# A decoder layer on one core: seven edits at the places where the matmul engine stops

## The chip, the cores and the metric

The kernel runs on one core of a Trainium2 chip. Its engines are named as in the profile: PE multiplies matrices, PEld loads its weights, DVE, ACT and POOL are the vector, scalar and general engines, SP issues transfers. The metric is the device time in microseconds (µs), the median of several executions. Times inside the program are counted from the start of the profiled span.

## The reference

One step of a hybrid decoder layer for 512 prompt tokens and 64 sample tokens (8 sequences of 8), all in float32, width 1024:

```python
u = _rms(x) * g_pre_mix
z, xbc, dt_raw, q, k, v, ig, fg, og = split(u @ w_in)
y_ssd = ssd_scan(silu(causal_conv(xbc)), softplus(dt_raw), ...)    # Mamba-2
h_ml = mlstm_scan(q, k, v, ig, log_sigmoid(fg), ...)               # gates per token
x = x + _rms(concat(y_ssd, h_ml) @ w_out) * g_post_mix
u = _rms(x) * g_pre_x
pr = softmax(einsum(u @ w_xq, mem_k))
x = x + _rms(einsum(pr, mem_v) @ w_xo) * g_post_x
u = _rms(x) * g_pre_ffn
x = x + _rms((silu(u @ w_gate) * (u @ w_up)) @ w_down) * g_post_ffn
```

`_rms(x)` divides each token's row by the root of its mean square. The outputs are x of both groups, the memory's keys and values, and the new states.

## The kernel before, in words

**Layout.** Activations lie with features on the 128 partitions and the 576 tokens (512 and 64) along the rows, eight blocks of 128 features. Tokens are taken in two halves, 256 and 320 (in the later stages 288 and 288), one bank of accumulators each.

**Products.** A float32 product is three matmuls of a reduced 32-bit format: high part by high part, high by low, low by high. A weight arrives by DMA in `raw` or `rawx`; ACT copies it to `whi` (the rounding copy is the high part), and DVE or POOL subtracts to get `wlo`; in other places ACT writes the negated high part and a DMA of POOL adds the weight to it (`wacc`, `wlo`). `split` (L196 on) is a cast on ACT and a subtraction on DVE, `split_w` (L178 on) does it for a weight with its load.

**Start.** 19 matmuls of zeros (`NWARM`, L309) run while the first loads are under way. Then, for each of eight blocks k, ACT makes `uh` and DVE `ul` from x (`xraw`), and two weight units `wi[0]`, `wi[1]` are split. For k = 0 x comes in two halves, and the weights are split behind both.

**Mixer.** The gates of the mLSTM are rows of 4 partitions that DVE and ACT work on beside the projection's matmuls; they are copied into one tile `r` (L545 to L567), which PE turns into columns (`ps_ct`, L589). In the state-space part, DVE makes `lm` from `ps_l`, ACT takes exponentials (L674), DVE multiplies (L675) and PE takes the product (`ps_yi`, L682). The mLSTM's values of the samples, `vts`, are taken out of their bank by a copy on ACT and an addition on DVE (L877, L878).

**Cross attention's output.** `xo` multiplies one block of features; `out` takes the squares for the norm and the scaled copy out of the bank, both on ACT (L270, L1560). PE writes the block three further on into the bank that is freed last.

**Feed-forward.** Products of two by two blocks take seven instead of eight part products (classes `Seven`, `Pair` for gate and up, `Down`), with sums of weights in `sw`: `parts2` casts a sum to `whi<-sw` on ACT and subtracts on DVE. The last 768 columns of the down projection are kept per block j in `wdh` and `wdl` (`w_of`).

**Tail.** The last stage is a list of steps with a place each (`at_`, then `plan.sort()`), issued in that order. `evac0(j)` adds a bank to `f_ffn`, squares it on ACT and scales it; `root` sums the squares over the partitions by matmuls with ones (`ps_ss`, one column per block of 128 tokens) and takes the square root on ACT, `root_end` refines it on DVE; `last` adds the scaled, transposed block to x and stores it; the last block is scaled on ACT and added on DVE (`scaled`, `scaled_add`).

**What sets the order.** Up to the tail, a scheduler orders each engine's instructions by its own simulated timeline, within what `issue_after` and priorities force. A small edit can so move instructions far from it. Each engine executes its own list in order.

Of the kernel before, what the change touches and what calls it, by code (L numbers as in the profile page):

```python
# [19 lines left out]
P = 128  # L20
T = 576
# [87 lines left out]
CCUT = 128  # L109
NWARM = 19  # L110
NSS = 7
# [4 lines left out]
def build(nc, tc, ctx, I, O):  # L116
# [52 lines left out]

    loads, casts, accs = [], [], []  # L170

# [5 lines left out]

    def split_w(src, n=1024, cut=CUT, acc=False, pool=None, to=None, raw=None):  # L178
# [89 lines left out]
    def add_sq(pool, ssq, src, j, w=T, eng=None, t0=0, q=None):  # L268
        if j == 0:
            A.activation(ssq[:, t0:t0 + w], src, AF.Square)  # L270
# [45 lines left out]
    for k in range(KT):  # L316
# [7 lines left out]
        if k == 0:  # L324
            with tc.issue_after(xd.ins), tc.high_priority(offset=300):

                A.activation(sp.tile([P, 1], F32, name="one"), wz[:, 0:1], AF.Exp)

        if k == 0:
            V.tensor_copy(wi[0][0][:, c], raws[0][:, c])  # L330
        for t0, n in ([(0, T)] if k else HALVES):
            ts_ = slice(t0, t0 + n)
            uhk = A.activation(uh[:, k, ts_], xraw[:, k, ts_], AF.Copy, scale=PAR("g_pre", k))
            ulk = V.scalar_tensor_tensor(ul[:, k, ts_], xraw[:, k, ts_], PAR("g_pre", k), uh[:, k, ts_].bitcast(F32),
                                         op0=ALU.mult, op1=ALU.subtract)
        if k % 2 == 0:
            for i in range(2):
                with tc.issue_after(uhk.ins), tc.issue_after(ulk.ins):
                    split(wi[i][0][:, c], wi[i][1][:, c], raws[i][:, c], cast=None if k or i else lambda *_: None)
    S.dma_start(c32, I["c32"][:, 0:NLONG])  # L340
# [4 lines left out]
    for k in range(KT):  # L345
        for (hi, lo), pss in zip(wi, ps0):
            wh, wl = hi[:, k * P:(k + 1) * P], lo[:, k * P:(k + 1) * P]
            for (t0, n), ps in zip(HALVES, pss):
                ah, al = U(k, t0, n), UL(k, t0, n)
                mm(ps, wh, ah, start=k == 0, stop=False)  # L350
                mm(ps, wh, al, start=False, stop=False)
                mm(ps, wl, ah, start=False, stop=k == KT - 1)
    with tc.issue_after(uhk.ins), tc.issue_after(ulk.ins):
# [212 lines left out]
    A.copy(r1[64:68, :], gpr[r4, :])  # L566
    A.copy(r1[96:100, :], sx[r4, :])  # L567
    A.copy(r2, mrw[r4, :])
# [271 lines left out]
    def values(g):  # L840
# [15 lines left out]
        def products(u, c, first, last):  # L856
# [18 lines left out]
            if n == TS:  # L875
                o = vts[:TS, 2 * g:2 * g + 2, 0:256]
                A.copy(o, p2[TS:P])  # L877
# [661 lines left out]
    def xo(j, i, pool=None):  # L1539
# [11 lines left out]
        def step(k0, k1):  # L1551
# [4 lines left out]
            evx.append(None)  # L1556

            def out():
                add_sq(ph, ssq, ps, j if i == 0 else XO1.index(j), n, t0=t0)
                evx[at_e] = A.activation(f[:, j, t0:t0 + n], ps, AF.Copy, scale=PAR("g_postx", j))  # L1560

# [266 lines left out]
    class Seven:  # L1828
# [85 lines left out]
    class Pair(Seven):  # L1914
# [8 lines left out]
        def done(s, a, i, ps, more=None):  # L1923
# [11 lines left out]
            V.tensor_tensor(g, g, ps, op=ALU.mult)  # L1935
            s.put(s.j + a, a, i, g)
# [197 lines left out]
    class Plain:  # L2134
# [3 lines left out]
        def put(s, j, a, i, g):  # L2138
            split(*[t_[:, j % 8, E[i]] for t_ in s.b], g)

# [40 lines left out]
    def root(name, terms, chunks):  # L2181

        n, ps = len(chunks), B0("ps_ss")
        for m, (t_, b) in enumerate(terms):
            for c, (t0, _) in enumerate(chunks):
                mm(ps[:, c:c + 1], t_[:, t0 - b:t0 - b + P], ones, start=m == 0 and c == 0, stop=m == len(terms) - 1, skip_group_check=True)
        v, y, a, r = few[:] if n == 3 else [fp.tile([P, n], F32, name=name + k) for k in ("_v", "_y", "_a", "_r")]
        w = fp.tile([P, n], F32, name=name + "_w")
        tail[name], tail["w", name] = (w, y, a, r), w
        V.tensor_scalar(v, ps[:, :n], 1.0 / 1024.0, EPS, op0=ALU.mult, op1=ALU.add)  # L2190
        A.activation(y, v, AF.Sqrt)
        V.reciprocal(tail["w", name], v)

    def root_end(name):
# [4 lines left out]
        V.scalar_tensor_tensor(r, r, 1.5, a, op0=ALU.add, op1=ALU.mult)  # L2199
        tail[name] = r  # L2200

# [10 lines left out]
    def evac0(j):  # L2212
        fj = f2[:, j, 0:256]
        V.tensor_tensor(fj, fj, tail[j], op=ALU.add)
        if j:
            squares[j] = ph.tile([P, 320], F32, name="sq", tag="sq", bufs=2)[:, :256]
        A.activation(squares[j] if j else ssqf[:, 0:256], fj, AF.Square)
        if j < 7:
# [49 lines left out]
    def last(i):  # L2268
        o, rc = xt[i][0], tail["pf0"][:, parts[i][0]:parts[i][0] + 1]
        V.scalar_tensor_tensor(o, ft[i], rc, o, op0=ALU.mult, op1=ALU.add)  # L2270
        store(i)
# [6 lines left out]
    def scaled():  # L2278
        tail["s"] = sw[:, 0:512].rearrange("p (j k) -> p j k", j=4)
        A.activation(tail["s"], ft[3], AF.Copy, scale=tail["pf0"][:, parts[3][0]:parts[3][0] + 1])  # L2280

    def scaled_add():
        V.tensor_tensor(xt[3][0], xt[3][0], tail["s"], op=ALU.add)
        store(3)
# [133 lines left out]
```

## Time and profile before

| what | value |
|---|---|
| median of 3 runs | 1079.3 µs (1079.01 to 1079.93) |
| profiled execution | 1077.81 µs |
| its span | 1075.9 µs |
| granted clock | 0.997 |
| PE busy | 1066.2 µs, 99% |
| DVE, ACT, POOL busy | 751.8, 607.6, 231.7 µs |

A row of the timeline has the start, the busy time, the engine, the line, the operation with its tiles, and in brackets how long the engine idled ahead of it and what ended that. A matmul's busy time is modelled and overlaps the next one's: PE's real pace is the distance from one start to the next. "x3" joins equal neighbours.

### The profile page before, as it was taken

The page shows a single profiled execution, that of the slowest core. Times are in us where ns is not written, and L with a number is a line of the kernel's source. Part 1 is how long each engine was busy: PE and PEld are TensorE (multiplying, and loading weights), DVE is VectorE, ACT ScalarE, POOL GpSimd, SP SyncE. Part 2 cuts the span into 40 slices and gives each one's busy share as a digit, 9 for nine tenths or more (in the row PEclk, how much of TensorE's full clock was granted, in tenths as well). Part 3 has the DMA queues.
Part 4 walks back from the last instruction along what each step waited for, and adds up shares of the span by engine and source line. Part 5 has one row for each costly group of instructions (what it writes and reads, how often), then busy time and mean ns, then how long its engine had stood idle before and what let it go on. Part 6 is the DMA issues. An engine that isn't in the chain of part 4 may idle for free.

```text
span 1075.9 us, 20705 instructions
## 1 busy us (share of the span) xinstructions
PE 1066.2 (99%) x8122; PEld 1013.8 (94%) x8122; DVE 751.8 (70%) x1509; ACT 607.6 (56%) x1094; POOL 231.7 (22%) x305
## 2 busy tenths in 40 slices
PE   9999999999999999999999999999999999999997
PEld 8999887778999999999999989999999999999997
DVE  6897775758877775559655555766467887787556
ACT  7778522345654556556555445545566566656653
POOL 1454543213213111000154201100011111111000
PEclk9999999999999999999999999999999999999998
DMA  6785544435655349643468775743476687578532
GB/s 208 177 161 131 157 138 166 147 85 172 197 148 150 107 131 341 234 168 116 143 212 286 266 256 171 252 127 94 133 180 142 156 201 165 116 190 185 128 132 89
DMA packets 58966, 181.76 MB, mean 169 GB/s; under 512 B 6604, under 2 KB 12108, under 8 KB 58356
## 3 DMA queue, kind: packets, MB, share of 16 engines
q1 hardware_dynamic: 42884, 138.22, 38.4%
q0 software_dynamic: 15408, 41.43, 19.3%
q8 instruction: 64, 1.05, 0.4%
q10 hardware_dynamic: 576, 0.79, 0.2%
q14 instruction: 34, 0.28, 0.1%
HBM read 159.75 MB, written 20.65 MB: 168 GB/s over the span
## 4 chain that ended last, share of the span: by engine, by line
PE 95%; DVE 3%; ACT 1%; issue 1%; DMA 0%; SPq 0%; DVEq 0%; ACTq 0%
PE ps_in L208 6%; PE ps_in L211 6%; PE ps_in L209 6%; PE ps_v L854 5%; PE ps_o L211 3%; PE ps_g L1910 3%; PE ps_g L1909 3%; PE ps_o L209 3%; PE ps_g L1911 3%; PE ps_o L208 3%; PE ps_u L1910 3%; PE ps_u L1911 3%; PE ps_u L1909 3%; PE ps_dn L1909 2%; PE ps_dn L1910 2%; PE ps_dn L1911 2%
## 5 line engine op out<-in xcount | busy, mean ns | idle before, releaser
L208 PE MATMUL ps_in<-uh,whi 128*128 128x320 f32 (+1 forms) x544 | 161.7, 297 | 0.0
L211 PE MATMUL ps_in<-uh,wlo 128*128 128x320 f32 (+1 forms) x544 | 161.7, 298 | 0.0
L209 PE MATMUL ps_in<-ul,whi 128*128 128x320 f32 (+1 forms) x544 | 161.0, 296 | 0.0
L186 ACT CAST whi<-raw 128x1024 fp32r<-128x1024 f32 (+1 forms) x104 | 105.3, 1014 | 94.3 <-PE ps_in L209 27.7
L193 DVE TENSOR_TENSOR wlo<-raw,whi 128x1024 fp32r<-128x1024 f32 (+2 forms) x97 | 94.7, 978 | 59.6 <-ACT whi L186 58.7
L211 PEld LDWEIGHTS ps_in<-uh,wlo 128*128 128x128 f32 x544 | 102.1, 188 | 2.0 <-issue 1.3
L208 PEld LDWEIGHTS ps_in<-uh,whi 128*128 128x128 f32 x544 | 102.3, 188 | 1.7 <-issue 0.8
L209 PEld LDWEIGHTS ps_in<-ul,whi 128*128 128x128 f32 x544 | 102.3, 188 | 0.4
L191 POOL DMA_DIRECT2D wlo<-win x31 | 27.0, 872 | 78.0 <-ACT wlo L190 65.5
L1909 PE MATMUL ps_g<-b,whi 128*128 128x288 f32 x144 | 42.5, 295 | 0.0
L1910 PE MATMUL ps_g<-b,whi 128*128 128x288 f32 x144 | 42.4, 295 | 0.0
L1910 PE MATMUL ps_u<-b,whi 128*128 128x288 f32 x144 | 42.2, 294 | 0.0
L1909 PE MATMUL ps_u<-b,whi 128*128 128x288 f32 x144 | 42.2, 294 | 0.0
L1882 ACT CAST whi<-rawx 128x1024 fp32r<-128x1024 f32 (+1 forms) x26 | 25.7, 988 | 27.6 <-PE ps_dn L1910 13.7
L198 DVE TENSOR_TENSOR wlo<-sw,whi 128x1024 fp32r<-128x1024 f32 (+1 forms) x26 | 29.6, 1140 | 15.0 <-ACT whi L197 14.9
L208 PE MATMUL ps_xo<-qh,whi 128*128 128x288 f32 x128 | 38.4, 302 | 0.1
L209 PE MATMUL ps_xo<-ql,whi 128*128 128x288 f32 x128 | 37.7, 296 | 0.0
L211 PE MATMUL ps_o<-mixm_h,wlo 128*128 128x256 f32 (+1 forms) x128 | 37.7, 295 | 0.0
L209 PE MATMUL ps_o<-mixm_l,whi 128*128 128x256 f32 (+1 forms) x128 | 37.5, 293 | 0.0
L211 PE MATMUL ps_xq<-u2h,wlo 128*128 128x320 f32 (+1 forms) x128 | 37.5, 294 | 0.0
L211 PE MATMUL ps_o<-mixs_h,wlo 128*128 128x320 f32 (+1 forms) x128 | 37.4, 292 | 0.0
L209 PE MATMUL ps_xq<-u2l,whi 128*128 128x320 f32 (+1 forms) x128 | 37.4, 294 | 0.0
(770 smaller groups left out, 3842.2 us busy)
## 6 DMA issues: line engine op xcount, KB each, us to landing
raw<-win SPq DMA_DIRECT2D x35, 512.0 KB, 4.2
raw<-wout SPq DMA_DIRECT2D x17, 512.0 KB, 4.4
raw<-wxq SPq DMA_DIRECT2D x13, 512.0 KB, 3.9
raw<-wgate SPq DMA_DIRECT2D x13, 512.0 KB, 3.5
raw<-wup SPq DMA_DIRECT2D x13, 512.0 KB, 4.8
wlo<-win POOLq DMA_DIRECT2D x24, 256.0 KB, 5.1
kva<-vc SPq DMA_DIRECT2D x11, 512.0 KB, 6.6
raw<-wv SPq DMA_DIRECT2D x10, 512.0 KB, 4.3
```

Source lines behind the costliest of these rows:

```text
L186: casts.append(A.copy(hi[:, :n], raw[:, :n]))
L191: accs.append(G.dma_start(lo[:, a:b], src[:, a:b], accum_op=ALU.add))
L193: e.tensor_tensor(lo[:, a:b], raw[:, a:b], hi[:, a:b].bitcast(F32), op=ALU.subtract)
L198: (eng or V).tensor_tensor(lo, src, hi.bitcast(F32), op=ALU.subtract)
L208: mm(ps, wh, ah, start=i == 0, stop=False)
L209: mm(ps, wh, al, start=False, stop=False)
L211: m = mm(ps, tiles[order[c]][1], xh(order[c], t0, n), start=False, stop=c == len(tiles) - 1)
L854: mm(ps, a, b, skip_group_check=True, **kw)
L1882: A.copy(s.h3[:, s.all], s.r2[:, s.all])
L1909: mm(ps, wh, b[0][k], start=start and k == 0, stop=False, skip_group_check=True)
L1910: mm(ps, wh, b[1][k], start=False, stop=False, skip_group_check=True)
L1911: m = mm(ps, wl, b[0][k], start=False, stop=k == nk - 1, skip_group_check=True)
```

## The change

The edits, in the order of the program:

- `NWARM` 19 becomes 17. For k = 0 the first half of x and both weights are split ahead of the second half, and PE takes the first halves of both units before the second halves.
- The copy of `sx` into `r` is made in two parts, of 256 and 320 tokens.
- In the second group, the copy of `vts` is issued behind the exponential number 13.
- The first block of `xo` is scaled on DVE, and ACT only squares it.
- In `Down`, `parts2` casts in two halves.
- In `w_of` the first `wdl` is made in two halves, block 2's ahead of block 1's and behind a product of gate and up, block 3's `wdh` behind the last cast of `hh`.
- In the tail the last add and squares go by 128 tokens; the root of the first block of tokens stays on ACT and DVE, that of the second is made on POOL (`pow` and four steps); the last addition is half on POOL, half on DVE.

```diff
-NWARM = 19
+NWARM = 17
...
         if to:
-            split(*to, raw[:, :n])
+            with tc.issue_after(after.ins) if after else ExitStack():
+                A.copy(to[0], raw[:, :n])
+            with tc.issue_after(behind.ins) if behind else ExitStack():
+                for a in range(0, n, piece or n):
+                    b = a + (piece or n)
+                    wlows.append(V.tensor_tensor(to[1][:, a:b], raw[:, a:b], to[0][:, a:b].bitcast(F32), op=ALU.subtract))
             return to
...
         if k == 0:
             V.tensor_copy(wi[0][0][:, c], raws[0][:, c])
-        for t0, n in ([(0, T)] if k else HALVES):
...
+            x_parts(*HALVES[0])
+            V.tensor_tensor(wi[0][1][:, c], raws[0][:, c], wi[0][0][:, c].bitcast(F32), op=ALU.subtract)
+            h, l = w_parts(1)
+            with tc.issue_after(h.ins), tc.issue_after(l.ins):
+                uhk, ulk = x_parts(*HALVES[1])
+        else:
+            uhk, ulk = x_parts(0, T)
...
+        for i, h in ((0, 0), (1, 0), (0, 1), (1, 1)) if k == 0 else ((0, 0), (0, 1), (1, 0), (1, 1)):
...
-    A.copy(r1[96:100, :], sx[r4, :])
+    for t0, n in HALVES:
+        A.copy(r1[96:100, t0:t0 + n], sx[r4, t0:t0 + n])
...
                 o = vts[:TS, 2 * g:2 * g + 2, 0:256]
-                A.copy(o, p2[TS:P])
+                with tc.issue_after(exps[13].ins) if g else ExitStack():
+                    A.copy(o, p2[TS:P])
...
+            if (j, i) == (0, 0):
+                V.tensor_scalar(f[:, j, t0:t0 + n], ps, PAR("g_postx", j), None, op0=ALU.mult)
+
             def out():
-                add_sq(ph, ssq, ps, j if i == 0 else XO1.index(j), n, t0=t0)
-                evx[at_e] = A.activation(f[:, j, t0:t0 + n], ps, AF.Copy, scale=PAR("g_postx", j))
+                e = add_sq(ph, ssq, ps, j if i == 0 else XO1.index(j), n, t0=t0)
+                evx[at_e] = e if (j, i) == (0, 0) else A.activation(f[:, j, t0:t0 + n], ps, AF.Copy, scale=PAR("g_postx", j))
...
-            split(s.h2[:, s.all], s.l2[:, s.all], sw[:, s.all])
+            for c in (s.LB, s.LA) if isinstance(s, Down) else [s.all]:
+                A.copy(s.h2[:, c], sw[:, c])
+            V.tensor_tensor(s.l2[:, s.all], sw[:, s.all], s.h2[:, s.all].bitcast(F32), op=ALU.subtract)
...
         if j not in kept:
+            behind = {}
+            if j == 2:
+                behind[2] = last.product
+            if j == 1:
+                w_of(2)
+                behind[1] = wlows[-1]
...
-            kept[j] = split_w(src, 768, 768, raw=raw, to=None if j > 4 else (wdh[:, j, :], wdl[:, j, :]))
+            kept[j] = split_w(src, 768, 768, raw=raw, to=None if j > 4 else (wdh[:, j, :], wdl[:, j, :]),
+                              piece=384 if j == 0 else None, behind=behind.get(j), after=stores[-1].cast if j == 3 else None)
...
+        if n == 2:
+            v, y, a, r = [fp.tile([P, 1], F32, name=name + k) for k in ("_v1", "_y1", "_a1", "_r1")]
+            V.tensor_scalar(v, ps[:, 1:2], 1.0 / 1024.0, EPS, op0=ALU.mult, op1=ALU.add)
+            G.tensor_tensor(y, v, C32("nhalf")[:, :1], op=ALU.pow)
+            G.tensor_tensor(a, y, y, op=ALU.mult)
+            G.tensor_tensor(a, a, v, op=ALU.mult)
+            G.tensor_scalar(a, a, -0.5, 1.5, op0=ALU.mult, op1=ALU.add)
+            G.tensor_tensor(r, a, y, op=ALU.mult)
+            tail["r", 1] = r
...
-        V.tensor_tensor(fj, fj, tail[j], op=ALU.add)
...
+        for c in [slice(0, 256)] if j < 7 else [slice(0, P), slice(P, 256)]:
+            V.tensor_tensor(fj[:, c], fj[:, c], tail[j][:, c], op=ALU.add)
+            A.activation(o[:, c], fj[:, c], AF.Square)
...
-        V.tensor_tensor(xt[3][0], xt[3][0], tail["s"], op=ALU.add)
+        for e, j in ((G, slice(0, 2)), (V, slice(2, 4))):
+            e.tensor_tensor(xt[3][0][:, j], xt[3][0][:, j], tail["s"][:, j], op=ALU.add)
```

The scheduler's order has moved at many places. Three of them follow; the rows have the line (the line numbers of the changed kernel are its own), the operation, its tiles and its shape.

PE, mixer, where the gates' columns are made: from the last matmul of the 256 half to the first `ps_ct`. Before:

```order
L211 MATMUL ps_in<-uh,wlo 128x256
L208 MATMUL ps_in<-uh,whi 128x320
L209 MATMUL ps_in<-ul,whi 128x320
L211 MATMUL ps_in<-uh,wlo 128x320
L208 MATMUL ps_in<-uh,whi 128x320
L209 MATMUL ps_in<-ul,whi 128x320
L211 MATMUL ps_in<-uh,wlo 128x320
L208 MATMUL ps_in<-uh,whi 128x320
L209 MATMUL ps_in<-ul,whi 128x320
L211 MATMUL ps_in<-uh,wlo 128x320
L208 MATMUL ps_in<-uh,whi 128x320
L589 MATMUL ps_ct<-c_78,r_1256 128x100
```

And now:

```order
L216 MATMUL ps_in<-uh,wlo 128x256
L213 MATMUL ps_in<-uh,whi 128x320
L214 MATMUL ps_in<-ul,whi 128x320
L216 MATMUL ps_in<-uh,wlo 128x320
L213 MATMUL ps_in<-uh,whi 128x320
L214 MATMUL ps_in<-ul,whi 128x320
L216 MATMUL ps_in<-uh,wlo 128x320
L213 MATMUL ps_in<-uh,whi 128x320
L214 MATMUL ps_in<-ul,whi 128x320
L611 MATMUL ps_ct<-c_78,r_1254 128x100
```

Ten matmuls of 320 columns stood ahead of `ps_ct`, now eight do; the other two follow its group.

ACT, mixer, second group, where the samples' values are taken (`lm` is the exponential). Before:

```order
L881 ACTIVATE vt_1796<-ps_v,rx_r 128x2x256
L674 ACTIVATE lm<-lm 128x512
L877 COPY vts<-ps_v 64x2x256
L674 ACTIVATE lm<-lm 128x512
L186 CAST whi<-raw 128x1024
L879 ACTIVATE vts<-vts,rx_r 64x2x256
```

And now:

```order
L904 ACTIVATE vt_1795<-ps_v,rx_r 128x2x256
L696 ACTIVATE lm<-lm 128x512 x2
L900 COPY vts<-ps_v 64x2x256
L191 CAST whi<-raw 128x1024
L195 ACTIVATE wlo<-whi 128x512
L902 ACTIVATE vts<-vts,rx_r 64x2x256
```

The two exponentials stand together, the copy behind them.

ACT, feed-forward, one Pair after the first group of Downs (`whi<-sw` is the cast of the summed weight). Before:

```order
L197 CAST hh_10321<-gt 128x288
L197 CAST whi<-sw 128x1024
L1856 ACTIVATE wlo<-rawx 128x512
L197 CAST u3h<-d_10721 128x4x128
L1929 ACTIVATE gt<-gt 128x288
L1949 COPY ct<-ps_u 128x288
L1942 COPY cc<-ps_g 128x288
```

And now:

```order
L202 CAST hh_10324<-gt 128x288
L202 CAST u3h<-d_10724 128x4x128
L1882 ACTIVATE wlo<-rawx 128x512
L1957 ACTIVATE gt<-gt 128x288
L1977 COPY ct<-ps_u 128x288
L1896 CAST whi<-sw 128x1024
L1970 COPY cc<-ps_g 128x288
```

The cast of the summed weight has moved behind four instructions.

More of the change, by code (lines that the diff above doesn't have):

```diff
@@ L167, in build @@
     ident, ones = C32("ident"), C32("ones")
-    loads, casts, accs = [], [], []
+    loads, casts, accs, wlows = [], [], [], []
     def hi_lo(pool=None):
@@ L176, in hi_lo, with split_w @@
         return hi, (pool or wp).tile([P, 1024], F32R, name="wlo", tag="wlo", bufs=NWX if pool else 3)
-    def split_w(src, n=1024, cut=CUT, acc=False, pool=None, to=None, raw=None):
+    def split_w(src, n=1024, cut=CUT, acc=False, pool=None, to=None, raw=None, piece=None, behind=None, after=None):
         if raw is None:
@@ L327, in build, with x_parts, w_parts @@
                 A.activation(sp.tile([P, 1], F32, name="one"), wz[:, 0:1], AF.Exp)
+        def x_parts(t0, n):
+            ts_ = slice(t0, t0 + n)
+            return (A.activation(uh[:, k, ts_], xraw[:, k, ts_], AF.Copy, scale=PAR("g_pre", k)),
+                    V.scalar_tensor_tensor(ul[:, k, ts_], xraw[:, k, ts_], PAR("g_pre", k), uh[:, k, ts_].bitcast(F32),
+                                           op0=ALU.mult, op1=ALU.subtract))
+        def w_parts(i):
+            hi, lo, raw = wi[i][0][:, c], wi[i][1][:, c], raws[i][:, c]
+            h = (A.copy if k or i else V.tensor_copy)(hi, raw)
+            return h, V.tensor_tensor(lo, raw, hi.bitcast(F32), op=ALU.subtract)
         if k == 0:
             V.tensor_copy(wi[0][0][:, c], raws[0][:, c])
-        for t0, n in ([(0, T)] if k else HALVES):
[L332 to L337, printed above, removed]
+            x_parts(*HALVES[0])
[5 more added lines that the diff above has]
+            uhk, ulk = x_parts(0, T)
+            if k % 2 == 0:
                 with tc.issue_after(uhk.ins), tc.issue_after(ulk.ins):
-                    split(wi[i][0][:, c], wi[i][1][:, c], raws[i][:, c], cast=None if k or i else lambda *_: None)
+                    w_parts(0)
+                    w_parts(1)
     S.dma_start(c32, I["c32"][:, 0:NLONG])
@@ L345, in build @@
     for k in range(KT):
-        for (hi, lo), pss in zip(wi, ps0):
+        for i, h in ((0, 0), (1, 0), (0, 1), (1, 1)) if k == 0 else ((0, 0), (0, 1), (1, 0), (1, 1)):
+            (hi, lo), (t0, n), ps = wi[i], HALVES[h], ps0[i][h]
             wh, wl = hi[:, k * P:(k + 1) * P], lo[:, k * P:(k + 1) * P]
-            for (t0, n), ps in zip(HALVES, pss):
-                ah, al = U(k, t0, n), UL(k, t0, n)
+            ah, al = U(k, t0, n), UL(k, t0, n)
+            with tc.issue_after(first.ins) if k == 0 and h else ExitStack():
                 mm(ps, wh, ah, start=k == 0, stop=False)
                 mm(ps, wh, al, start=False, stop=False)
-                mm(ps, wl, ah, start=False, stop=k == KT - 1)
+                m = mm(ps, wl, ah, start=False, stop=k == KT - 1)
+            if k == 0 and h == 0:
+                first = m
     with tc.issue_after(uhk.ins), tc.issue_after(ulk.ins):
@@ L2138, in put @@
         def put(s, j, a, i, g):
-            split(*[t_[:, j % 8, E[i]] for t_ in s.b], g)
+            s.cast = split(*[t_[:, j % 8, E[i]] for t_ in s.b], g)
     for n_, j0 in enumerate((10, 16)):
@@ L2268, in last @@
     def last(i):
-        o, rc = xt[i][0], tail["pf0"][:, parts[i][0]:parts[i][0] + 1]
+        o, rc = xt[i][0], tail["r", parts[i][0]]
         V.scalar_tensor_tensor(o, ft[i], rc, o, op0=ALU.mult, op1=ALU.add)
@@ L2279, in scaled @@
         tail["s"] = sw[:, 0:512].rearrange("p (j k) -> p j k", j=4)
[L2280 removed]
+        A.activation(tail["s"], ft[3], AF.Copy, scale=tail["r", 1])
     def scaled_add():
[L2283 removed]
+        for e, j in ((G, slice(0, 2)), (V, slice(2, 4))):
+            e.tensor_tensor(xt[3][0][:, j], xt[3][0][:, j], tail["s"][:, j], op=ALU.add)
         store(3)
```

18 lines of the change are left out of this document (9 added, 9 removed).

## The prediction

> **What bounds the kernel now.** Read first the page's busy times, then the list of waits for PE, then the timeline around each stop.
>
> ```profile
> PE 1066.2 (99%) x8122; PEld 1013.8 (94%) x8122; DVE 751.8 (70%) x1509; ACT 607.6 (56%) x1094; POOL 231.7 (22%) x305
> ...
> PE ps_in L350 <- ACT uh L333: 0.8, 1, 0.8
> PE ps_yi L682 <- DVE lm L675: 0.3, 1, 0.3
> ```
>
> PE is busy for 1066.2 of 1075.9 µs, and no matmul is removed. The change can gain only where PE stops, or in the few microseconds ahead of the first and behind the last matmul. Of the stops the list of waits names only the longest, since the modelled end of a matmul (0.28 to 0.31 behind its start) hides the first 0.2 of a stop; the others are found by the distance from one start to the next. Seven places come out of that, in µs from the span's start: 6, 79, 239, 635, 843 with a twin at 943, 1029 to 1031, and the tail. The change has an edit for each. SP's and POOL's loads keep their order.
>
> **Start: first weights, and two warm-ups fewer.**
>
> ```profile
> 1.06 4.24 PE L309 MATMUL ps_warm<-wz 128*128 128x256 bf16 x19 [1.06 <-DVE wz L306]
> 6.37 0.68 PE L350 MATMUL ps_in<-uh,whi 128*128 128x320 f32 x2 [0.84 <-ACT uh L333]
> 10.08 0.28 PE L351 MATMUL ps_in<-ul,whi 128*128 128x256 f32 x1
> 1.17 0.47 ACTq L323 DMA_DIRECT2D raw<-win  x1
> raw<-win ACTq DMA_DIRECT2D x1, 128.0 KB, 3.0
> 5.75 0.56 ACT L333 ACTIVATE uh<-xraw,par 128x320 fp32r<-128x320 f32 x1 [1.81 <-DMA xraw<-xT]
> 6.22 0.39 ACT L197 CAST whi<-raw 128x256 fp32r<-128x256 f32 x1
> 8.81 0.82 DVE L334 SCALAR_TENSOR_TENSOR ul<-xraw,par,uh 128x576 fp32r<-128x576 f32 x1 [0.51 <-ACT uh L333]
> ```
>
> The second weight lands 3.0 after its issue at 1.17, at about 4.2, but its cast waits until 6.22 behind an activation that waits for x. Now the cast (0.39) and both low parts come first, and six 256-wide matmuls fit into the hole ahead of 6.37, in which PE idles for 0.84. The hole itself stays: the 320 half of x lands no sooner. What is late next is ul of k=2, ready at 8.81+0.82 = 9.63. Its first matmul started at 10.08 and can start at about 9.70, so **0.38** is the most that this point lets through and what I take (0 to 0.45, as a later load could hold PE instead). The two warm-ups, 4.24/19 = 0.22 each, end where nothing was ready; they give nothing of their own.
>
> **The gates' row in two parts.**
>
> ```profile
> 78.81 0.67 ACT L567 COPY r<-sx 4x576 f32<-4x576 f32 x1
> 78.96 0.31 PE L211 MATMUL ps_in<-uh,wlo 128*128 128x320 f32 x1
> 79.10 0.31 PE L208 MATMUL ps_in<-uh,whi 128*128 128x320 f32 x1
> 79.62 0.28 PE L589 MATMUL ps_ct<-c,r 100*128 100x100 f32 x1 [0.21 <-ACT r L567]
> ```
>
> PE starts ps_ct 0.52 behind its predecessor, where a matmul of 320 columns follows in 0.14: 0.38 lost. The first part, 256 of 576 columns, takes an estimated 0.40 on ACT by the 0.39 of the cast above, so ps_ct could start at about 79.35, 0.27 sooner. But the order of PE has moved too: two 320-wide matmuls that stood ahead of ps_ct now stand behind it, and they cost 0.29 there. The stop comes earlier and no shorter: **0** (-0.1 to +0.1).
>
> **Samples' values behind an exponential.**
>
> ```profile
> 236.88 0.59 ACT L877 COPY vts<-ps_v 64x512 f32<-64x512 f32 x1
> 238.11 0.68 DVE L675 TENSOR_TENSOR lm<-lm,cbs 128x512 f32<-128x512 f32 x1
> 238.35 0.28 PE L211 MATMUL ps_in<-uh,wlo 128*128 128x256 f32 x1
> 238.93 0.88 PE L682 MATMUL ps_yi<-lm,xdt 128*64 128x128 f32 x12 [0.30 <-DVE lm L675]
> ```
>
> A 256-wide matmul is followed in about 0.12 when PE runs; here 0.58 pass, 0.46 lost. With the copy (0.59) out of the way, the second exponential ends about half a microsecond sooner and DVE's lm follows it, for the addition of the values now comes behind. That removes the stop. The new order puts the next pair of ps_l one and three 320-wide matmuls later, and their chain through lm to the next ps_yi had nothing to spare; I give one matmul back, 0.15: **0.30** (0.15 to 0.46). The copy's own readers come microseconds later.
>
> **First output of the cross attention through DVE.**
>
> ```profile
> 634.21 0.41 ACT L270 ACTIVATE ssqxo<-ps_xo 128x288 f32<-128x288 f32 x1
> 634.51 0.49 ACT L1560 ACTIVATE f_xo<-ps_xo,par 128x288 f32<-128x288 f32 x1
> 634.64 0.29 PE L211 MATMUL ps_xo<-qh,wlo 128*128 128x288 f32 x1
> 635.06 0.40 PE L208 MATMUL ps_xo<-qh,whi 128*128 128x288 f32 x1
> ```
>
> PE needs the bank that f_xo empties at 635.00. With that step on DVE, squaring is the last reader and ends at 634.62, before PE asks at 634.64+0.13. PE wins the gap, 0.42-0.13 = 0.29, and the longer matmul behind a stop, 0.40 instead of 0.29. Together 0.40; I take **0.38** (0.2 to 0.39). DVE's added step, of the size of the 0.49 beside it, would come at the worst half of that late.
>
> **Cast of the summed weight in two halves.**
>
> ```profile
> 842.38 0.84 ACT L197 CAST whi<-sw 128x768 fp32r<-128x768 f32 x1 [0.65 <-PE ps_dn L1910]
> 842.92 0.29 PE L1911 MATMUL ps_dn<-te,wlo 128*128 128x288 f32 x1
> 843.27 0.41 PE L1909 MATMUL ps_dn<-hh,whi 128*128 128x288 f32 x1
> 943.24 0.41 PE L1909 MATMUL ps_dn<-hh,whi 128*128 128x288 f32 x1
> ```
>
> PE waits for a cast that ends at 843.22; its own turn would be 843.05. Half of it, an estimated 0.50 between the 0.39 of 256 columns and 0.84 of 768, ends at 842.88. The gap is 842.92 to 843.27 less 0.13, so 0.22, and the matmul behind it is 0.11 longer (0.41 against 0.29): 0.33. The second pass of these loops shows the same long matmul at 943.24. Twice 0.33 less a little: **0.64** (0.5 to 0.65). The price is one more ACT instruction in each Down, and a reshuffle: in the Pairs the scheduler moves casts of the summed weight behind up to four others (shown above). PE's matmuls on them move back too, so I price that at nothing here and keep it as a rival.
>
> **Weights of the last chunk.**
>
> ```profile
> 1028.45 0.31 PE L209 MATMUL ps_dn<-hl,wdh 128*128 128x320 f32 x1
> 1028.80 0.41 PE L211 MATMUL ps_dn<-hh,wdl 128*128 128x320 f32 x1
> 1030.50 0.30 PE L209 MATMUL ps_dn<-hl,wdh 128*128 128x320 f32 x1
> 1030.86 0.56 PE L208 MATMUL ps_dn<-hh,whi 128*128 128x320 f32 x2
> 1031.87 0.84 ACT L197 CAST wdh<-raw 128x768 fp32r<-128x768 f32 x1 [1.06 <-DMA raw<-wdown]
> 1032.87 0.45 PE L208 MATMUL ps_dn<-hh,wdh 128*128 128x320 f32 x2
> ```
>
> Two stops of 0.21 and 0.22, with 0.10 behind each: 0.63. The first low part by halves, and gt and hh ahead of two weights, remove both. But two matmuls on, PE needs the cast that a load releases at 1031.87. That load is issued when the first weight's low part is done, which the split doesn't move. The cast ends at 1032.71 and PE takes it at 1032.87, so 0.12 is all the room, and a new stop there eats most: **0.05** (0 to 0.63).
>
> **Tail by blocks of 128 tokens.**
>
> ```profile
> 1068.73 0.16 DVE L2190 TENSOR_SCALAR pf_v<-ps_ss 128x2 f32<-128x2 f32 x1 [0.76 <-PE ps_ss L2186]
> 1069.84 0.69 ACT L2280 ACTIVATE sw<-ps_ft,pf_r 128x512 f32<-128x512 f32 x1 [0.72 <-DVE pf_r L2199]
> 1071.77 0.68 DVE L2283 TENSOR_TENSOR raw<-raw,sw 128x512 f32<-128x512 f32 x1
> L921 POOL TENSOR_TENSOR hn_y<-hn_v,c 128x1 f32<-128x1 f32 x2 | 1.1, 568 | 16.7 <-DVE hn_v L920 16.7
> L198 POOL TENSOR_TENSOR mk<-mko,mk 128x256 fp32r<-128x256 f32 x6 | 4.4, 739 | 3.7 <-ACT mk L197 3.7
> L1000 POOL TENSOR_TENSOR qpad<-qk,vt 128x32 f32<-128x32 f32 x8 | 1.8, 254 | 0.0
> 50.04 1.24 POOL L488 COPY convo<-cb 128x3 f32<-128x3 f32 x1
> ```
>
> Squares by halves bring pf_v forward by some 0.13, to 1068.60. The second block's v follows at about 1069.1, and POOL starts: a power 0.57 (the first row), four small steps at 0.25 (the third), so its r stands at about 1070.7. ACT scales (0.69), POOL adds its half (0.74, the second row), with 0.15 between them: the last store is issued at 1072.3, against 1071.77+0.68 = 1072.45 now. That would gain 0.15. The Trainium skill, "SBUF — State Buffer", section "Who interferes with whom", says that a DVE instruction with two SBUF inputs and a GpSimd one that reads SBUF exclude each other, the later one standing until the first is through; no run here shows it. By it DVE's half would wait for POOL's. One behind the other, as a mechanism of this kernel, the halves end at 0.74+0.4, and the tail loses 0.2 instead. I take **0**, between the two. The ends: with the 0.57 of the first row for all five steps, r stands at 1071.95 and the store comes 1.1 late; with POOL never late, DVE's own path is shorter by 0.13 and half an addition of 0.68, some 0.4.
>
> **The rivals.** *All the upper ends*: nothing holds PE behind the removed stops, and POOL's small steps take 0.1: 0.45+0.1+0.46+0.39+0.65+0.63+0.4 = 3.1, 1076.2 µs. For it: each stop has an edit, and most loads are released by PE itself, so that they come sooner with it. Against it: the load at 1031.87 and the order at 79. *POOL decides the end, and the kernel is slower*: POOL steps are not steady. The copy of 128x3 took 1.24 at 50.04. Five such steps put r at 1069.1+6.2 = 1075.3 and the last store at 1076.9, 4.4 late: 1079.3-1.75+4.4 = 1082.0. It turns the sign from 1.75 late, and passes the bound below from 3.9. *Moved casts stop PE*: each cast that comes too late costs 0.33, as at 843; ACT's order has 26 of them, and 13 stops are 4.3: 1079.3-1.75+4.3 = 1081.9. Against it: PE's order moves with them.
>
> **How the numbers follow.** The sum is 0.38+0+0.30+0.38+0.64+0.05+0 = 1.75. The profiled execution took 1077.81, its span 1075.9 and 1.9 around it; it is 1.5 below the median of the timed runs. So 1076.1 in a profile, and 1079.3-1.75 = 1077.5 as a median. About 0.2%, 2.2 µs, is what a measurement of this kernel can tell from no change. Forecast 0.45 (its own range 1076.9 to 1078.6, from the ends of the tail and of the start; 0.10 of it over the bound), upper ends 0.35, POOL 0.10, casts 0.10. Faster 0.10+0.35 = 0.45, same 0.35, slower 0.20. The range reaches from a little under the upper ends, 1075.9, to 1080.5, part of the way into the slow cases.
>
> **What would show it.** The first 320-wide matmul still at about 6.4 and the next part of k=2 near 9.7; ps_ct still named among the waits; no stop at 239, 635, 843 and 943; a wait for wdh near 1032; the last store within half a microsecond of where it was, behind the last matmul. Wrong, if PE stops at new places in the feed-forward, or if POOL's chain ends after 1073 less the gain before it.

## The result, and the profile after

| kernel | median | runs | ratio to before |
|---|---|---|---|
| before | 1079.28 µs (1078.41 to 1080.13) | 16 | |
| after | 1081.57 µs (1080.05 to 1083.94) | 16 | 1.0021 [1.0015, 1.0028] |

The change makes the kernel slower, by 2.3 µs. The profiled execution of after took 1081.51, its span 1079.7, at a granted clock of 0.996 (0.997 before). It lies at its median, while the profiled execution of before lay 1.5 below its own; the two spans, 3.8 apart, overstate the difference.

The page's line of busy times and the list of waits for PE, of after:

```profile
PE 1065.9 (99%) x8120; PEld 1013.9 (94%) x8120; DVE 752.3 (70%) x1513; ACT 607.8 (56%) x1103; POOL 233.7 (22%) x311
...
PE ps_os L1467 <- ACT kva L1492: 1.1, 1, 1.1
PE ps_warm L314 <- DVE wz L311: 1.1, 1, 1.1
PE ps_in L369 <- ACT uh L336: 0.5, 1, 0.5
PE ps_dn L213 <- ACT wdh L184: 0.3, 1, 0.3
PE ps_ct L611 <- ACT r L589: 0.3, 1, 0.3
```

PE's busy time is what it was (1066.2). The wait for `lm` is gone, that for `wdh` is new, as forecast; a wait of 1.1 for `kva` at 601 is one that nothing forecast. But PE is only 0.45 behind before at 1060, and 0.32 at its last matmul (1069.02 against 1068.70): the loss lies behind it.

The timeline of after, from the root of the second block of tokens to the last addition:

```profile
1069.33 0.14 DVE L2230 TENSOR_SCALAR pf_v<-ps_ss 128x1 f32<-128x1 f32 x1
1069.55 0.57 POOL L2231 TENSOR_TENSOR pf_y<-pf_v,c 128x1 f32<-128x1 f32 x1 [44.07 <-DVE pf_v L2230]
1070.20 0.19 POOL L2232 TENSOR_TENSOR pf_a<-pf_y 128x1 f32<-128x1 f32 x1
...
1071.03 0.19 POOL L2235 TENSOR_TENSOR pf_r<-pf_a,pf_y 128x1 f32<-128x1 f32 x1
1071.25 0.69 ACT L2326 ACTIVATE sw<-ps_ft,pf_r 128x512 f32<-128x512 f32 x1 [1.80 <-POOL pf_r L2235]
...
1072.01 0.72 POOL L2330 TENSOR_TENSOR raw<-raw,sw 128x256 f32<-128x256 f32 x1 [0.80 <-ACT sw L2326]
1072.08 0.93 DVE L2330 TENSOR_TENSOR raw<-raw,sw 128x256 f32<-128x256 f32 x1
```

POOL's chain is steady: 0.57 and four steps of 0.19, each 0.27 behind the last. The last store is issued at 1073.09, 0.61 later than before (1072.48), and yet the span ends 3.8 later. What stands behind the last store is seen in the instructions of the kernel's closing line, which are not counted as busy and do not stand in the timeline. The answer for that line gives for each kind how many, the shortest, median and longest in ns, and the start of the first and the last. Before:

```profile
L2413 POOLq DRAIN  x3: 46/102/6379, 1024.9 to 1075.7; - x3
L2413 SPq DRAIN  x3: 7/7/7, 1075.1 to 1075.4; - x3
```

After:

```profile
L2460 POOLq DRAIN  x3: 46/102/6967, 1072.0 to 1079.5; - x3
L2460 SPq DRAIN  x3: 7/7/7, 1075.6 to 1079.2; - x3
```

And SP's waits at that line (in all, times, longest), before and after:

```profile
SPq L2413 <- PEq L2413: 0.7, 2, 0.5
```

```profile
SPq L2460 <- PEq L2460: 4.0, 2, 3.5
```

At its end each engine runs a DRAIN, an instruction that here ends only behind the engine's last work, and the closing barrier waits for all. POOL's takes microseconds: 6.38 before, from 1024.9, when its last instruction (a memset of 0.15 at 1024.88) had just been issued; it was over at 1031.2, with 40 µs of PE's work to hide it. Now POOL has work until 1072.73, so its DRAIN runs from 1071.98 to 1078.94. SP had seen the last store land and was ready at 1075.65. It then stands for 3.5 in one wait, where it stood for 0.5. The list names PE there, whose own DRAIN took 0.8 from 1068.5 on; by the times it is POOL's that came last, for it ends at 1078.94 and SP goes on at 1079.2.

### The profile page after: what moved, and what is told of

It reads as the page before. It is cut to its first block, busy times and chain, and to the rows that moved or that the text cites. A ratio compares the mean times of both kernels' runs of the same rounds, so it can differ in the third digit from the quotient of the medians.

```text
span 1079.7 us, 20726 instructions
## 1 busy us (share of the span) xinstructions
PE 1065.9 (99%) x8120; PEld 1013.9 (94%) x8120; DVE 752.3 (70%) x1513; ACT 607.8 (56%) x1103; POOL 233.7 (22%) x311
## 4 chain that ended last, share of the span: by engine, by line
PE 91%; DMA 3%; DVE 3%; ACT 1%; POOL 1%; issue 1%; SPq 0%; DVEq 0%; ACTq 0%
PE ps_in L213 6%; PE ps_in L216 6%; PE ps_in L214 5%; PE ps_v L876 5%; PE ps_o L216 3%; PE ps_g L1938 3%; PE ps_g L1937 3%; PE ps_o L214 3%; PE ps_o L213 3%; PE ps_g L1939 3%; PE ps_u L1938 3%; PE ps_u L1939 3%; PE ps_u L1937 3%; PE ps_dn L1937 2%; PE ps_dn L1939 2%; PE ps_dn L1938 2%
## 5 line engine op out<-in xcount | busy, mean ns | idle before, releaser
L191 ACT CAST whi<-raw 128x1024 fp32r<-128x1024 f32 (+1 forms) x104 | 105.3, 1014 | 96.4 <-PE ps_in L214 29.3
L1887 ACT CAST whi<-raw 128x1024 fp32r<-128x1024 f32 (+1 forms) x26 | 25.6, 985 | 22.7 <-PE ps_g L1938 11.8
L213 PE MATMUL ps_o<-mixs_h,whi 128*128 128x320 f32 (+1 forms) x128 | 37.5, 293 | 0.0
```

What stands on the lines that cost most here:

```text
L213: mm(ps, wh, ah, start=i == 0, stop=False)
L1887: s.c1 = A.copy(s.h1[:, s.all], s.r1[:, s.all])
```

## The experiments

Three theories for the loss: T1, POOL's closing DRAIN; T2, POOL's chain, through the last store alone; T3, the new stops of PE. The first four kernels tell them apart.

**The tail without POOL.** After, with the root and the last addition as before (`root` for both blocks of tokens on ACT and DVE, below the addition); the squares by 128 tokens and all else stay. Of the diff against after, the part of the addition:

```diff
-        for e, j in ((G, slice(0, 2)), (V, slice(2, 4))):
-            e.tensor_tensor(xt[3][0][:, j], xt[3][0][:, j], tail["s"][:, j], op=ALU.add)
+        V.tensor_tensor(xt[3][0], xt[3][0], tail["s"], op=ALU.add)
```

> The changed kernel with the root of both blocks and the whole last addition on ACT and DVE, as before; squares by halves and all other edits stay. Theory 1 (POOL's closing drain, which ran until 1078.95 in the changed kernel, takes about 6.2 us from POOL's last instruction on and holds the end): some 3.3 less than the changed kernel, 1078.3. Theory 2 (POOL's chain only makes the last store late, by 0.3 beside PE's own 0.3): 0.3 less, 1081.3. Theory 3 (the time went at 601 us, in the memory's weights, and in the feed-forward): no change, 1081.6.

Measured: 1078.78 µs (10 runs), ratio to before 0.9998 [0.9989, 1.0008]. T1's 1078.3 is nearest: POOL's share in the tail cost 2.8 of after's 1081.57 (before has the same median, 1079.28, in both sets). T2 and T3 allowed 0.3 at most, and T3 falls with this kernel, which keeps every edit ahead of the tail. What is left of the change gains 0.5 by the medians, 0.2 by the ratio, and the interval holds no gain as well.

**Before, with POOL's half of the last addition alone.**

```diff
-        V.tensor_tensor(xt[3][0], xt[3][0], tail["s"], op=ALU.add)
+        for e, j in ((G, slice(0, 2)), (V, slice(2, 4))):
+            e.tensor_tensor(xt[3][0][:, j], xt[3][0][:, j], tail["s"][:, j], op=ALU.add)
```

> The kernel before with nothing but half of the last addition on POOL. Theory 1: POOL's last instruction ends near 1071.4 of the span, the drain near 1077.6, the span near 1078.6: 2.7 more than before, 1082.0. Theory 2: the addition itself changes the last store by less than 0.3, so 1079.0 to 1079.6. Theory 3: as before, 1079.3.

Measured: 1080.83 µs, ratio 1.0015 [1.0005, 1.0025]. That is above all that T2 and T3 allow, and 1.2 below T1's 1082.0, which lies at the upper end of the interval. The two halves in the timeline:

```profile
1071.06 0.72 POOL L2284 TENSOR_TENSOR raw<-raw,sw 128x256 f32<-128x256 f32 x1 [45.58 <-ACT sw L2280]
...
1072.21 0.41 DVE L2284 TENSOR_TENSOR raw<-raw,sw 128x256 f32<-128x256 f32 x1
```

And POOL's DRAIN, of 6.97 from 1071.0:

```profile
L2414 POOLq DRAIN  x3: 46/102/6972, 1071.0 to 1078.5; - x3
```

The last store is issued 3.56 behind the start of PE's last matmul, 0.2 sooner than before, and SP is ready for the end no later behind that matmul (6.48, before 6.47); yet the kernel is slower. T2 falls: one instruction of 0.72 on POOL holds the end.

**After, with the root on POOL and the addition on DVE.** Its diff against after is the part shown for the first experiment, alone.

> The changed kernel with the whole last addition on DVE; the root of the second block stays on POOL, whose last instruction then ends at about 1071.2 instead of 1072.7. Theory 1: the drain ends 1.5 sooner, so 1080.1. Theory 2: the last store moves by 0.2 at most, 1081.4 to 1081.8. Theory 3: 1081.6.

Measured: 1080.96 µs, ratio 1.0017 [1.0007, 1.0026]. The interval, 1080.0 to 1082.1, holds what all three theories say, and the median is nearer to T2's 1081.4 than to T1's 1080.1; so the time does not tell them apart. The trace does: POOL ends with a step of 0.19, and its DRAIN reaches 1.96 past the moment when SP is ready, where it reached 3.29 in after.

**Before, with a small POOL instruction ahead of the tail's end.**

```diff
+    at_(7.05, lambda: G.tensor_copy(few[0][:, 0:3], f2[:, 6, 0:3]))
```

> The kernel before with one more POOL instruction, a copy of 128x3 behind the next to last block's squares, at about 1065. Theory 1, with a drain that counts from POOL's last instruction: it is over near 1071.5, before the others have finished, and nothing changes: 1079.3. If instead any POOL instruction in the last stage makes the closing drain long, some 3 more: 1082. Theories 2 and 3: 1079.3.

Measured: 1079.77 µs, ratio 1.0003 [0.9993, 1.0012]; span 1075.9, as before. The copy in the timeline, and POOL's DRAIN at the closing line:

```profile
1065.18 0.18 POOL L2301 COPY pf_v<-f_ffn 128x3 f32<-128x3 f32 x1 [40.19 <-ACT f_ffn L2219]
```

```profile
L2414 POOLq DRAIN  x3: 46/93/6417, 1065.2 to 1075.6; - x3
```

So the DRAIN counts from POOL's last instruction, whatever it is, and costs only what reaches past the stores. From the traces, in µs:

| kernel | POOL's last ends | its DRAIN ends | SP is ready | span |
|---|---|---|---|---|
| before | 1025.03 | 1031.24 | 1075.17 | 1075.95 |
| copy at 1065 | 1065.37 | 1071.58 | 1075.12 | 1075.89 |
| root on POOL | 1072.04 | 1078.25 | 1076.29 | 1079.04 |
| half addition | 1071.78 | 1077.99 | 1075.62 | 1078.78 |
| after | 1072.73 | 1078.94 | 1075.65 | 1079.74 |

Column two to three is 6.21 in all five; the span ends 0.77 to 0.80 behind the later of columns three and four. In the seven other profiles POOL's last is the memset near 1025, and the 6.21 is the same. T1 is shown: POOL's last instruction must end some 6.2 µs ahead of the moment when the last store has landed. Why its DRAIN takes that long no run here tells.

That leaves the forecast gain of 1.75, of which 0.5 came by the medians. Three kernels hold its parts, three more test a cause.

**Before, with three parts of the change**: the first output of `xo` through DVE, the cast in halves, the last squares by 128 tokens. The edits are those of the change.

> Before, with three parts of the change: first output of the cross attention through DVE, the cast of the summed weight in halves, the last squares by halves; the tail is otherwise as before, and nothing of POOL stands behind 1025. Theory 'terms': these parts give what the trace of after shows, 0.38 at 635, 0.18 at each of 843 and 943, and some 0.13 at the last squares: 0.87 in all, 1078.4 us, span 1075.1 if nothing ahead of 600 differs. PE still stops two matmuls behind the first use of the summed weight, by some 0.10, since the cast's second half ends only then. Theory 'forecast': 0.33 at each cast, 1.17 in all, 1078.1 us, and no stop at 844. Rival 'casts': the moved casts cost elsewhere, no gain, 1079.3.

Measured: 1077.57 µs (12 runs), before 1078.66 in the same set; ratio 0.9992 [0.9984, 1.0001]. PE's distance to before, at the same matmul: from +0.52 to +0.14 at 636, from +0.11 to -0.07 at 844, from -0.06 to -0.24 at 944, and 0.13 more at the last squares (-0.22 at 1060, but the last matmul 0.35 sooner). These are the sizes in after too, and theory 'terms' holds. But at 422 this kernel lost 0.6, far ahead of its first edit (below).

**The same, with the samples' values behind the exponential and the cast in three pieces.**

```diff
-            for c in (s.LB, s.LA) if isinstance(s, Down) else [s.all]:
+            for c in (s.LB, slice(0, P), slice(P, s.n)) if isinstance(s, Down) else [s.all]:
```

> As the last kernel, with the samples' values behind the exponential, and the cast of the summed weight in three pieces (its upper half, 128 columns, the other 256). Theory 'terms': the stop two matmuls behind the first use goes, 0.10 more at each of 843 and 943; and the values' 0.30 at 239 is there at 400 but no longer at 605, as the weights of the stretch from 550 to 605 come at the pace of the DMA engines and a sooner PE waits for them: 0.87+0.2 = 1.07, 1078.2 us. Rival 'values kept': 0.30 more of it stays to the end, 1.37, 1077.9 us, span 1074.5.

Measured: 1078.11 µs, ratio 0.9995 [0.9986, 1.0004]. By the distance to before 0.30 is won at 844 and 0.30 at 944. After's timeline shows why its halves won only 0.18:

```profile
843.17 0.93 ACT L1896 CAST whi<-sw 128x384 fp32r<-128x384 f32 x2 [0.65 <-PE ps_dn L1938]
...
843.85 0.29 PE L1937 MATMUL ps_dn<-hh,whi 128*128 128x288 f32 x1
843.98 0.29 PE L1938 MATMUL ps_dn<-hl,whi 128*128 128x288 f32 x1
...
844.16 0.40 PE L1937 MATMUL ps_dn<-hh,whi 128*128 128x288 f32 x1
```

The first half is there in time. The second is wanted two matmuls on, and ends at 843.17+0.93 = 844.10, later than a whole cast of 0.84 would. PE stops for 0.05, and the long matmul behind a stop comes with it. With three pieces, of 1.02 together, no long one stands there:

```profile
843.64 1.02 ACT L1874 CAST whi<-sw 128x384 fp32r<-128x384 f32 x3 [0.67 <-PE ps_dn L1916]
...
844.31 0.30 PE L1915 MATMUL ps_dn<-hh,whi 128*128 128x288 f32 x1
844.45 0.29 PE L1916 MATMUL ps_dn<-hl,whi 128*128 128x288 f32 x1
...
844.58 0.29 PE L1915 MATMUL ps_dn<-hh,whi 128*128 128x288 f32 x1
```

The cast's part of theory 'terms' holds, 0.12 more at each place. Whether the values' gain stays is not told: the median is no better than that of the kernel with halves, and this profile lost 0.7 at 422 and 0.6 at 445, both times waiting for `f_mix`.

**Before, with the start, the gates' row and the values alone.**

> Before, with the other three parts ahead of 600: the start with two warm-ups fewer and the first weights first, the gates' row in two parts, the samples' values behind the exponential. Theory 'loads': at 9 the kernel stands where before stands, within what the landing of x differs from run to run (0.3); the gates' row costs 0.13 to 0.2 at 79; the values gain 0.30 at 239; at 605 no lead is left, and a stop for the copy behind the load of wmv may stand at 601: 1079.3 to 1079.5 us. Theory 'forecast': 0.38+0+0.30 = 0.68 sooner, 1078.6 us, at every point behind 240.

Measured: 1078.58 µs, ratio 0.9995 [0.9986, 1.0004]. At the start nothing is gained, as theory 'loads' has it, though more is lost than its 0.3: at 40 this kernel stands 0.68 behind before, at 87 0.8, at 240 0.48, and 0.5 from there to the end. The values win 0.37. No lead was lost at 601, but this run had none to lose.

Profiled runs differ more at the start than the edit could give: at 40 the kernels with the start's edit stand at -0.03, 0.25, 0.68 and 1.74 against before, those without at 0.03, 0.19, 0.36, 0.58, 0.59, 0.65 and 2.00. Ten of the twelve profiles, before's among them, lie within 0.7. In these the second half of x's first block lands at 5.47 to 6.35, though not in the order of PE's positions, so that how much the landing makes is not shown. The two largest are not a matter of x, which lands at 6.24 and 6.16 there. At 2.00 stands the last kernel below, the cast out of the way with the parts. Of the same stretch, 8 to 9 µs, the view by windows has (busy time and instructions of PE, PEld, DVE, ACT, POOL, then PE's granted clock, and DMA), first in that kernel, then in before:

```profile
8.00:9.00 1.00, 1.00 (x6) 1.00 (x5) 0.91 (x3) 0.91 (x2) 0.00 (x0) 0.50 1.09 406
```

```profile
8.00:9.00 1.00, 1.00 (x9) 1.00 (x9) 0.49 (x2) 1.00 (x3) 0.00 (x0) 1.00 1.05 388
```

The clock stays at 0.50 until 11.4, and 3.4 µs at half the clock cost PE some 1.7. The tail without POOL (1.74) has the same pace until 10.35, 10 matmuls between 8 and 10 where before has 17, though the view shows no lower clock there. Whether fewer warm-ups make this likelier is open: it is one profile in four with them, one in eight without.

**Two stores less.** The second of the kernels above, without the stores of `o_mv` for two of four blocks.

```diff
-            S.dma_start(O["mv"][:, :, h * 256:(h + 1) * 256], mo)
+            if h not in (1, 2):
+                S.dma_start(O["mv"][:, :, h * 256:(h + 1) * 256], mo)
```

> As the last but one, without the stores of two of the four blocks of the memory's values (o_mv, at 563 and 591); those parts of that output are left unwritten. It tells whether the DMA engines set PE's pace from 550 to 605. Theory 'DMA': the load of wmv issued at 564 lands sooner, ACT waits less than 2.7 for the one of 591, no stop stands at 601, and a lead at 400 is still there at 605: 0.2 to 0.3 faster than with the stores, 1077.9 us. Rival: the lead is lost there in the same way, 1078.2 us; the stores were not in the way.

Measured: 1077.73 µs, ratio 0.9988 [0.9979, 0.9998], against 1078.11 with the stores: not to be told apart. No stop at 601, but in the kernel with the stores there was none either, and ACT still waits 3.84 for a load of `wmv` ahead of 600.56. Instead PE loses 0.7 at 626, where it waits for a load of `vc`, in this profile alone (its order has moved around there, too):

```profile
625.86 0.62 PE L1446 MATMUL ps_os<-kva 128*32 128x256 f32 x2 [0.64 <-DMA kva<-vc]
```

So the kernel settles nothing about the DMA engines' part.

**A cast out of the way at 422.** Of the ten profiles up to here four stop at 422 for 0.6 to 1.9, and the one of before does not. (The expectation below counts six of ten, from 0.25 up: with the stops at 406 in after, 0.26, and at 447 in the kernel with three pieces, 0.64, it is six stops, but in five profiles.) ACT's timeline, of before and of the kernel with three parts:

```profile
419.04 1.05 ACT L1215 CAST preh<-prel 128x1024 fp32r<-128x1024 f32 x1 [2.42 <-DMA prel<-wup]
419.99 1.04 ACT L186 CAST whi<-raw 128x1024 fp32r<-128x1024 f32 x1
420.94 0.69 ACT L1125 COPY f_mix<-ps_o 128x320 f32<-128x320 f32 x2
```

```profile
420.38 1.05 ACT L1215 CAST preh<-prel 128x1024 fp32r<-128x1024 f32 x1 [4.18 <-DMA prel<-wup]
421.34 1.05 ACT L186 CAST whi<-raw 128x1024 fp32r<-128x1024 f32 x1
422.29 0.68 ACT L1125 COPY f_mix<-ps_o 128x320 f32<-128x320 f32 x2
422.75 0.39 PE L208 MATMUL ps_o<-mixs_h,whi 128*128 128x256 f32 x1 [0.29 <-ACT f_mix L1125]
```

Two copies that free PE's banks stand behind a cast that waits for a load; where the load lands 1.3 later, PE stops. The edit makes that cast one output tile later, in two kernels: alone, and with the parts that gain (`xo` through DVE, the cast in three pieces, the values, the squares by 128 tokens).

```diff
-        while ahead:
+        while len(ahead) > (1 if turns else 0):
             n_, t_ = ahead.pop(0)
```

> Before, with nothing changed but the casts of the loads that are split ahead (preh<-prel), one output tile later, so that fewer copies of f_mix stand behind them on ACT. Theory 'luck': the profile of before is one without a stop at 422 and 601, 1.5 below the median; the median holds such stops, and this edit takes away most of those at 422: 0.4 below the before of the same chip, ratio 0.9996, no stop between 405 and 440. Rival 'edits': the stops at 422 came with the edits of the change and are not in the runs of before, so that nothing is gained here, ratio 1.0000 or above.

> Before, with the first output of the cross attention through DVE, the cast of the summed weight in three pieces, the samples' values behind the exponential, the last squares by halves, and the casts of the loads that are split ahead (preh<-prel, 405 to 440) one output tile later. Theory 'terms': 0.38 at 635, 0.30 at each of 843 and 943, 0.13 at the last squares, 0.1 at 239 (0.37 in the three of ten profiles in which the load of win lands late, nothing in the others), and 0.4 at 422, where ACT's copies of f_mix stand behind a cast that waits for a load and PE stops for 0.25 to 1.9 in six of ten profiles: 1.6 below the before of the same chip, ratio 0.9985. Rival 'loads': the loads stop PE elsewhere in the same stretch, 1.2 below, ratio 0.9989, with a stop between 405 and 440 in the profile.

Measured: alone 1078.47 µs against 1079.58 in the same set, ratio 0.9990 [0.9979, 1.0001]; with the parts 1077.59, ratio 0.9987 [0.9975, 0.9998]. Neither profile stops between 405 and 440 (the first loses 0.5 at 445), as theories 'luck' and 'terms' have it, and the second ratio is near the 0.9985 forecast; the first alone is not told from no change, nor are the two from each other. So the stop's cause at 422 is read from the rows above, and that it costs time in the median is not shown. The second is the one kernel with the whole computation that is measurably faster than before.

## Why the prediction was wrong

**Tail: the step that failed.** "I take 0, between the two", with ends of 1.1 late and 0.4 early. The chain itself was priced right: with PE's 0.45 at 1060 taken off, r stood at 1070.77 (1071.03+0.19-0.45) where 1070.7 was forecast, and the tail lost 0.16 up to the last store (0.61-0.45), within the ends. What was missing is the end behind the last store. The sum let the end follow the store, as it does before, and no term or rival held POOL's closing DRAIN, which was in the profile of before, 6.38 long at 1024.9. It cost 2.8 by the medians; in the profile of after it reaches 3.29 past SP (1078.94-1075.65). The sign that the prediction set for POOL, a chain that ends after 1073, did not show: POOL was through at 1072.73, and the time went behind it. The rival that POOL decides the end had the engine and the sign, but another cause: its steps of 1.24 did not come.

The rule that the tail was weighed against held. POOL's half took 0.72 in both kernels; DVE's took 0.41 when POOL had finished and 0.93 beside it. DVE's started at 1072.08 and POOL's was through at 1072.73, 0.65 on. That agrees with what the Trainium skill, "SBUF — State Buffer", section "Who interferes with whom", says of such a pair, and by it the tail was to lose 0.2 up to the last store; it lost 0.16. The fit is near and not exact: had DVE stood until POOL was through and then taken its 0.41, it would have taken 1.06, not 0.93.

**Start: the wrong limit, 0.38 forecast, nothing seen.** The six matmuls fill the hole as forecast. x landed later in that run, its second half at 5.92 (5.73 in before), as the timeline of after shows:

```profile
5.94 0.56 ACT L336 ACTIVATE uh<-xraw,par 128x320 fp32r<-128x320 f32 x1 [1.46 <-DMA xraw<-xT]
6.55 0.55 PE L369 MATMUL ps_in<-uh,whi 128*128 128x320 f32 x2 [0.50 <-ACT uh L336]
...
7.63 0.82 DVE L337 SCALAR_TENSOR_TENSOR ul<-xraw,par,uh 128x576 fp32r<-128x576 f32 x1 [0.55 <-ACT uh L336]
...
8.50 0.39 PE L370 MATMUL ps_in<-ul,whi 128*128 128x256 f32 x1
```

The term took `ul` of k=2 for what is late next. It is `ul` of k=1, ready at 7.63+0.82 = 8.45; PE's first matmul on it starts at 8.50. There it starts in before too, by PE's own pace, with `ul` ready at 8.30:

```profile
7.49 0.81 DVE L334 SCALAR_TENSOR_TENSOR ul<-xraw,par,uh 128x576 fp32r<-128x576 f32 x1
...
8.50 0.28 PE L351 MATMUL ps_in<-ul,whi 128*128 128x256 f32 x1
```

So this point had some 0.15 to give (8.30 and 0.05, instead of 8.50), and the later x took it. In the other two kernels with the edit that ran at full clock PE starts there 0.06 behind `ul` as well. The range for this term, 0 to 0.45, also took the landing of x as that of one run.

**Gates' row: right, 0.** The stop came sooner and no shorter:

```profile
78.78 0.31 PE L214 MATMUL ps_in<-ul,whi 128*128 128x320 f32 x1
78.89 0.76 ACT L589 COPY r<-sx 4x256 f32<-4x256 f32 x2
79.44 0.28 PE L611 MATMUL ps_ct<-c,r 100*128 100x100 f32 x1 [0.34 <-ACT r L589]
```

The first of the two copies took 0.40, as estimated, and `ps_ct` starts at 79.44 instead of 79.62, but its predecessor has moved up by more, from 79.10 to 78.78: 0.51 lost, where it was 0.38. That difference is within what differs from run to run: 0.32 to 0.50 in the eight profiles without the edit, 0.37 to 0.51 in the four with it.

**Samples' values: right for the profile, not for every run.** The stop at 239 is gone, 0.37, of which 0.07 is given back by 300, so 0.30. But in two kernels without this edit (the copy at 1065, the three parts) the stop is missing too. ACT's cast ahead of the exponentials tells them apart, first in before, then with the three parts:

```profile
234.05 1.05 ACT L186 CAST whi<-raw 128x1024 fp32r<-128x1024 f32 x1 [2.35 <-PE ps_v L854]
```

```profile
233.25 1.05 ACT L186 CAST whi<-raw 128x1024 fp32r<-128x1024 f32 x1 [1.26 <-PE ps_v L854]
```

In the half addition's profile the same cast waits 2.30 and names the load of `win`, which takes 4.9 from issue to landing in before and 3.7 with the three parts. The stop is there where the load lands about 1 µs later: in three of the five profiles without the edit.

**First output of xo: right.** 0.38 in after, and 0.37 or 0.38 in the six other kernels with the edit.

**Cast of the summed weight: mis-sized, 0.64 forecast, 0.36 measured.** The step took the end of the first half for the end of the stop; the second half was not priced. In three pieces the edit brings 0.60. The rival of moved casts that stop PE did not come.

**Last chunk: right.** Both stops are gone and a new one eats them, at the cast named:

```profile
1032.46 0.84 ACT L184 CAST wdh<-raw 128x768 fp32r<-128x768 f32 x1 [1.14 <-DMA raw<-wdown]
...
1033.35 0.41 PE L213 MATMUL ps_dn<-hh,wdh 128*128 128x320 f32 x1 [0.35 <-ACT wdh L184]
```

PE's distance to before is 0.45 on both sides of it.

**What the sum makes of it.** Terms as measured: start 0, gates 0, values 0.2 to 0.3, xo 0.38, casts 0.36, last chunk 0, squares 0.13: about 1.1 in place of 1.75. The kernel without POOL in the tail gained 0.5 by the medians (its interval, 0.9 slower to 1.2 faster, holds 1.1 too); POOL in the tail took 2.8; and 2.3 is what after lost. That these three fit proves nothing, since 0.5 and 2.8 come from one and the same median; the proof for POOL is the table of DRAINs. The stop at 601 of after's profile, 1.1 long, is not in this sum: of all the others only the copy at 1065 shows one, of 0.2.

```profile
601.27 1.05 ACT L191 CAST whi<-raw 128x1024 fp32r<-128x1024 f32 x1 [4.30 <-DMA raw<-wmv]
602.22 0.36 ACT L1492 COPY kva<-ps_pts 128x256 f32<-128x256 f32 x1
```

It is the picture of 422 again, a copy that frees PE behind a cast that waits for a load. Whether an earlier PE makes it likelier stays open: the copy at 1065 had a lead of 0.3 at 425 and had lost it by 603, but that is one run.

## What to carry to other kernels

Before giving a last step to an engine that had been idle, look at what that engine does behind its last instruction: the closing instructions are in the trace, though in no list of busy time, and here POOL's is 6.2 µs. Ask of every stop that an edit removes whether a load's landing made it; such a stop is in some runs only, and a profile 1.5 µs below its median may be a run without several of them. When a cast is cut, price the last piece against its own reader, not only the first.

## What the runs showed that was not expected

POOL's closing DRAIN ends 6.21 µs behind the end of POOL's last instruction, in all twelve traces, be that a memset of 0.15, a copy of 0.18, a step of 0.19 or an addition of 0.72. The other engines' are short: 7 ns on SP, 8 to 152 on ACT in before, and DVE's of up to 1.9 µs (1.1 in after) and PE's of 0.9 end with their own last additions and matmuls. The Trainium skill, "VectorE: DVE Perf Modes", section "The DRAIN you can't avoid", gives the DRAINs that the runtime puts ahead of and behind a kernel as some 12 ns on all five engines. Those here stand at a line of the program and are not the same ones; a reader who takes that figure for them is wrong for POOL by 6 µs.

PE's position at 40 µs varies by 2.0 from profile to profile, the size of the whole change: by 0.7 in ten profiles, and in two by about as much as 3 to 4 µs at half PE's pace cost, with a granted clock of 0.50 in the one of them whose view shows it.
